# Two-block transformer net on one core: two more granules in the mixer's filler, raw room opened before the up projection, and reciprocal roots taken in twos

## The chip, the cores and the metric

One core of one Trainium2 chip runs the whole program as one kernel. The metric is the device time of one execution in microseconds (us). The engines are TensorE (PE, its weight loads PEld), VectorE (DVE), ScalarE (ACT), GpSimd (POOL) and SyncE (SP), whose queue issues the transfers.

## What is computed

Two blocks on x of 1024 tokens by 1024 columns, in fp32. The change touches the first block, from the mixer's output to the gate behind the MLP:

```
mixed = (gate_attn * y_attn + gate_conv * y_conv) @ w_o
x = x + rms_norm(mixed, g_post_mix)
h = rms_norm(x, g_pre_mlp)
f = square(relu(h @ w_up)) @ w_down          # 1024 -> 4096 -> 1024
x = x + rms_norm(f, g_post_mlp)
x = x + sigmoid(rms_norm(x, g_ple) @ w_ple_gate) * (p @ w_ple_proj)
```

with rms_norm(x, g) = x * rsqrt(mean(x * x) + 1e-6) * g. Before it stand attention, a short convolution and the input projection; behind it a block with memory attention and two mixers. The change leaves their code alone.

## The kernel before

Every fp32 product is three matmuls on rounded halves: an operand is split into hi (ACT, L104 and L112) and lo = x - hi (POOL for weights, L105; DVE for activations, L113), and hi*hi, lo*hi and hi*lo are added in PSUM (L124 to L126). act_hi and act_lo hold the activations of all 1024 tokens. The order of the instructions on each engine isn't written out: a scheduler sets it when the program is built, from the order of the calls, its estimates of durations, and the pools, whose buffers a later tile can have only when the earlier one's readers are done.

**Mixer's way out** (`out_stage`). For each tile of 128 tokens the product with w_o (r_o, L751 to L753), the sum of squares, the reciprocal root, the residual, the next norm, and a transpose on PE (tp, L178) into act_hi and act_lo. A *filler* stands among the last tiles: plain granules of the up projection. A granule is 128 of the 4096 columns; half a granule (j, h) is 24 matmuls on 512 tokens, in ps_f. Half h = 0 needs only tiles 0 to 3, so it can run while tiles 4 to 7 are still normed. Before, the filler is the h = 0 halves of granules 0 and 1.

**Up projection** (`up`). Six more plain halves of granules 0 to 3, then 14 pairs of granules by a scheme of seven products instead of eight (`seven`, in the order 1, 2, 3, 6, 7, 5, 4, each 12 matmuls, in ps_s). Its operands are sums of weight quarters (S, wS_hi, wS_lo, made in `weights`) and of token quarters B: T1, T2, T3 (`token_sums`, DVE operations on 128x2048, made in tiles Tf and split into T_hi and T_lo), and T4 (`last_sum`, made in a tile S and split into B[0, 1]'s own place in act_hi and act_lo). Products 5, 6, 7 and 4 use T1, T2, T3 and T4; products 3 and 7 use the weights' sum S34. ReLU and square give f_out, which goes to DRAM (f_rows_up), one transfer of 128x1024 for each granule.

**Down projection** (`down`). f_raw(j) is loaded from f_rows_up (`load_f`) and split into slot (j + 4) % 8 of act_hi and act_lo, whose token quarters the pairs still read; two granules at a time are multiplied with w_down into ps_d and added to acc. The pool of f_raw, two of 128x1024, is opened with down's other pools, behind those of up.

**Last tiles.** With granules 30 and 31, `after(t)` runs `final(t)`: sum of squares of acc(t) (ACT, L163), reciprocal root q1 (`rstd`, ten DVE operations on 128x1, L143 and L152 to L158), gain (POOL L988, DVE L989), scaling by q1 and adding of x_f (ACT L992, POOL L993, DVE L994); then the sum of squares and the root of the tile t - 1, now with its residual, and its norm xn (L974 to L977), which `turn` transposes for the gate's product (ps_pg).

Of the kernel before, what the change touches and what calls it, by code (L numbers as in the profile page):

```python
# [8 lines left out]
F32 = mybir.dt.float32  # L9
# [3 lines left out]
AF = mybir.ActivationFunctionType  # L13
ALU = mybir.AluOpType
# [14 lines left out]
class Net:  # L29
# [109 lines left out]
    def rstd(self, ss, n):  # L139

        v = self.nc.vector
        x, y, t, u = (self.sm.tile([P, 1], F32, name=f"rstd_{k}") for k in "xytu")
        v.tensor_scalar(out=x, in0=ss, scalar1=1.0 / n, scalar2=EPS, op0=ALU.mult, op1=ALU.add)  # L143
        if self.use_sqrt:
            self.nc.scalar.activation(out=t, in_=ss, func=AF.Sqrt, scale=1.0 / n, bias=self.eps)
            v.reciprocal(out=y, in_=t)
            v.scalar_tensor_tensor(out=t, in0=y, scalar=x, in1=y, op0=ALU.mult, op1=ALU.mult)
            v.tensor_scalar(out=u, in0=t, scalar1=-0.5, scalar2=1.5, op0=ALU.mult, op1=ALU.add)
            v.tensor_tensor(out=y, in0=y, in1=u, op=ALU.mult)
            return y  # L150

        v.tensor_scalar(out=y.bitcast(I32), in0=x.bitcast(I32), scalar1=-0.5, scalar2=float(0x5F3759DF),  # L152
                        op0=ALU.mult, op1=ALU.add)
        for _ in range(2):
            v.scalar_tensor_tensor(out=t, in0=y, scalar=x, in1=y, op0=ALU.mult, op1=ALU.mult)
            v.tensor_scalar(out=u, in0=t, scalar1=0.375, scalar2=-1.25, op0=ALU.mult, op1=ALU.add)
            v.tensor_tensor(out=u, in0=u, in1=t, op=ALU.mult)
            v.scalar_tensor_tensor(out=y, in0=u, scalar=1.875, in1=y, op0=ALU.add, op1=ALU.mult)  # L158
        return y
# [619 lines left out]
    def up(self, st):  # L779


        nc, tc, a = self.nc, self.tc, self.a
        v = nc.vector
        hi, lo = self.act_hi, self.act_lo
        col = lambda k: slice(k * P, (k + 1) * P)
        fp = st.enter_context(tc.tile_pool(name="fo", bufs=1))
        fo = {}

        def leave(j, h):
            if h == 0 or not fo[j][1]:  # L790
                fo[j][1] = True
                return
            nc.sync.dma_start(out=self.fd[j], in_=fo[j][0])

        def out_of(j):
            if j not in fo:
                fo[j] = [fp.tile([P, S], F32, name="f_out", tag=f"f{j % 2}"), False]
            return fo[j][0]

        def plain(j, w, h, psm):  # L800
            ps = psm.tile([P, H], F32, name="ps_f", tag="r")
            self.proj_T(ps, w, col, (hi, lo), 8, h)
            o = out_of(j)[:, h * H:h * H + H]
            nc.scalar.activation(out=o, in_=ps, func=AF.Relu)
            v.tensor_tensor(out=o, in0=o, in1=o, op=ALU.mult)
            leave(j, h)

        def up_w(js):
            return [(j, self.split_w(a["w_up"][j], 1024)) for j in js]

        w01 = []

        def filler(psm):
            w01.extend(up_w([0, 1]))
            for j, w in w01:
                plain(j, w, 0, psm)

        self.out_stage(a["w_o"], a["g_post_mix"], a["g_pre_mlp"], a["x"], self.xd, filler)
# [8 lines left out]
        def rec(out, b):  # L827
            v.tensor_tensor(out=out, in0=b[0].bitcast(F32), in1=b[1].bitcast(F32), op=ALU.add)

        def sub(out, x, y):  # L830
            v.tensor_tensor(out=out, in0=x, in1=y, op=ALU.subtract)

        def token_sums():

            with tc.tile_pool(name="tf", bufs=1) as tf:
                f1, f2, f3 = (tf.tile([P, 4, H], F32, name=f"Tf{n}") for n in (1, 2, 3))
                rec(f1, B[0, 0])
                rec(f3, B[0, 1])
                sub(f1, f3, f1)
                self.split(*T[1], f1)  # L840
                rec(f2, B[1, 1])
                sub(f3, f2, f3)
                sub(f2, f2, f1)
                self.split(*T[2], f2)
                self.split(*T[3], f3)

        def last_sum():

# [28 lines left out]

        def seven(j, ops):

            o11, o12, o21, o22 = (out_of(j + i)[:, h * H:h * H + H] for i in range(2) for h in range(2))  # L880
            k1, u2 = (kp.tile([P, H], F32, name=n) for n in ("k1", "u2"))
            ps = {}

            def add(out, n, more):
                v.tensor_tensor(out=out, in0=ps[n], in1=more, op=ALU.add)

            def done(o, i):
                v.scalar_tensor_tensor(out=o, in0=o, scalar=0.0, in1=o, op0=ALU.max, op1=ALU.mult)
                leave(j + i, 1)

            for n in (1, 2, 3, 6, 7, 5, 4):
                ps[n] = psm.tile([P, H], F32, name=f"ps_s{n}", tag="r")
                (sh, sl), a0, (mh, ml) = ops[n]
                self.mm3(ps[n], [((sh[:, col(a0 + k)], sl[:, col(a0 + k)]), (mh[:, k], ml[:, k])) for k in range(4)])
                if n == 1:
                    nc.scalar.activation(out=k1, in_=ps[n], func=AF.Copy)
                elif n == 2:
                    add(o11, 2, k1)
                    done(o11, 0)
                elif n == 6:  # L900
                    add(u2, 6, k1)
                elif n == 7:
                    add(o21, 7, u2)
                elif n == 5:
                    add(o12, 5, u2)
                    add(o22, 5, o21)
                    add(o12, 3, o12)
                    done(o22, 1)
                    done(o12, 0)
                elif n == 4:  # L910
                    add(o21, 4, o21)
                    done(o21, 1)

        w23 = up_w([2, 3])
        pairs = list(range(4, 32, 2))
        plains = [(j, w, 1) for j, w in w01] + [(j, w, h) for h in range(2) for j, w in w23]
        for n, (j, w, h) in enumerate(plains):
            plain(j, w, h, psm)
            if n == 0:
                token_sums()  # L920
        kp = st.enter_context(tc.tile_pool(name="kept", bufs=2))
        sf = st.enter_context(tc.tile_pool(name="sf", bufs=1))
        wu = st.enter_context(tc.tile_pool(name="wu", bufs=2))
        ahead = weights(4)
# [7 lines left out]
    def mlp(self):  # L932
# [4 lines left out]
        act = (hi, lo)  # L937
        col = lambda k: slice(k * P, (k + 1) * P)
        self.fd = self.dram.tile([32, P, S], F32, name="f_rows_up")
        with ExitStack() as st:  # L940
            self.up(st)
        with ExitStack() as st:
            f2 = st.enter_context(tc.tile_pool(name="f2", bufs=2))
            fp = st.enter_context(tc.tile_pool(name="fp", bufs=2))
            fs = {}
# [678 lines left out]
```

## Time and profile before

| | |
|---|---|
| median of three runs | 2968.9 us (2965.43 to 2971.95) |
| the profiled execution | 2973.59 us |
| its span, first to last instruction | 2971.8 us |
| mean granted TensorE clock | 0.972 of full speed |
| busy: PE, PEld, DVE, ACT, POOL | 93%, 78%, 57%, 41%, 34% |
| moved by DMA | 311.14 MB, 105 GB/s in the mean |

Times within a row of the timeline are counted from the span's start. A matmul is listed with its own length, in which the next one already runs, so the pace is read from start to start. "[2.22 <-DVE act_lo L113]" behind an instruction is the idle time of its engine before it and what ended it. The granted clock of a stretch is 1.00 at 2.4 GHz and 0.50 at 1.2 GHz.

### The profile page before, as it was taken

The page shows a single profiled execution, that of the slowest core. Times are in us where ns is not written, and L with a number is a line of the kernel's source. Part 1 is how long each engine was busy: PE and PEld are TensorE (multiplying, and loading weights), DVE is VectorE, ACT ScalarE, POOL GpSimd, SP SyncE. Part 2 cuts the span into 40 slices and gives each one's busy share as a digit, 9 for nine tenths or more (in the row PEclk, how much of TensorE's full clock was granted, in tenths as well). Part 3 has the DMA queues.
Part 4 walks back from the last instruction along what each step waited for, and adds up shares of the span by engine and source line. Part 5 has one row for each costly group of instructions (what it writes and reads, how often), then busy time and mean ns, then how long its engine had stood idle before and what let it go on. Part 6 is the DMA issues. An engine that isn't in the chain of part 4 may idle for free. (4 is left out here: it accounts for less than half of the span.)

```text
span 2971.8 us, 37779 instructions
## 1 busy us (share of the span) xinstructions
PE 2774.5 (93%) x13490; PEld 2312.0 (78%) x13490; DVE 1692.0 (57%) x3201; ACT 1218.9 (41%) x2368; POOL 995.9 (34%) x823
## 2 busy tenths in 40 slices
PE   7999999998999998999989899689989999999988
PEld 5888778877878887888867689677768978778867
DVE  6320288845387665666587435287872426666643
ACT  5111266642442222121144423377763535555543
POOL 4221111113345442223255212332324344455442
PEclk9999999998999999999989899799999999999999
DMA  5111211127323335323123322632344232222162
GB/s 206 50 44 63 75 56 55 61 70 263 109 77 122 108 106 193 108 90 109 43 82 144 116 87 71 184 116 92 112 142 168 99 112 65 72 72 73 49 234 93
DMA packets 130644, 311.14 MB, mean 105 GB/s; under 512 B 14796, under 2 KB 34892, under 8 KB 130456
## 3 DMA queue, kind: packets, MB, share of 16 engines
q1 hardware_dynamic: 130456, 308.72, 31.0%
q8 instruction: 107, 1.75, 0.2%
q14 instruction: 81, 0.66, 0.1%
HBM read 213.33 MB, written 85.38 MB: 101 GB/s over the span
## 5 line engine op out<-in xcount | busy, mean ns | idle before, releaser
L105 POOL TENSOR_TENSOR w_lo<-w_raw,w_hi 128x1024 fp32r<-128x1024 f32 (+5 forms) x220 | 452.8, 2067 | 1057.8 <-ACT w_hi L104 1055.6
L104 ACT ACTIVATE w_hi<-w_raw 128x1024 fp32r<-128x1024 f32 (+5 forms) x220 | 192.5, 886 | 407.2 <-PE ps L125 90.7
L124 PE MATMUL ps_m<-act_hi,w_hi 128*128 128x512 f32 x716 | 289.8, 405 | 28.6 <-ACT w_hi L104 11.6
L125 PE MATMUL ps_m<-act_lo,w_hi 128*128 128x512 f32 x716 | 283.9, 397 | 0.0
L126 PE MATMUL ps_m<-act_hi,w_lo 128*128 128x512 f32 x716 | 282.4, 396 | 0.0
L113 DVE TENSOR_TENSOR pl<-tp_at,ph 128x512 fp32r<-128x512 f32 (+3 forms) x416 | 222.8, 560 | 85.9 <-ACT ph L112 83.8
L112 ACT ACTIVATE ph<-tp_at 128x512 fp32r<-128x512 f32 (+3 forms) x416 | 196.8, 500 | 106.2 <-PE tp_at L299 95.8
L1017 DVE TENSOR_TENSOR acc<-ps_d,acc 128x512 f32<-128x512 f32 x240 | 161.9, 687 | 109.7 <-PE ps_d L126 109.7
L299 PE MATMUL tp_at<-ident,p 128*128 128x128 f32 x1280 | 204.2, 275 | 16.1 <-DVE pl L113 5.7
L254 ACT ACTIVATE p<-p,mx 128x256 f32<-128x256 f32 (+7 forms) x256 | 180.3, 706 | 81.9 <-DVE mx L243 50.3
L124 PE MATMUL ps_d<-w_hi,act_hi 128*128 128x512 f32 x512 | 202.4, 395 | 7.7 <-ACT act_hi L112 7.7
L125 PE MATMUL ps_d<-w_lo,act_hi 128*128 128x512 f32 x512 | 202.0, 395 | 0.0
L126 PE MATMUL ps_d<-w_hi,act_lo 128*128 128x512 f32 x512 | 199.4, 392 | 0.0
L299 PEld LDWEIGHTS tp_at<-ident,p 128*128 128x128 f32 x1280 | 152.1, 140 | 48.5 <-DVE pl L113 9.1
L124 PEld LDWEIGHTS ps_m<-act_hi,w_hi 128*128 128x128 f32 x716 | 136.8, 191 | 64.8 <-ACT w_hi L104 12.7
L751 PE MATMUL r_o<-w_hi,act_hi 128*128 128x512 f32 x384 | 151.1, 403 | 20.5 <-DVE ga L687 7.9
L126 PEld LDWEIGHTS ps_m<-act_hi,w_lo 128*128 128x128 f32 x716 | 136.0, 190 | 28.6
L125 PEld LDWEIGHTS ps_m<-act_lo,w_hi 128*128 128x128 f32 x716 | 136.9, 191 | 25.9
L291 PE MATMUL o_ps<-ph,v 128*128 128x512 f32 (+3 forms) x400 | 145.5, 364 | 8.5 <-ACT ph L112 4.3
L753 PE MATMUL r_o<-w_hi,act_lo 128*128 128x512 f32 x384 | 151.7, 396 | 0.0
L752 PE MATMUL r_o<-w_lo,act_hi 128*128 128x512 f32 x384 | 151.3, 396 | 0.0
L292 PE MATMUL o_ps<-pl,v 128*128 128x512 f32 (+3 forms) x400 | 146.7, 374 | 0.4 <-DVE pl L113 0.2
(389 smaller groups left out, 6938.1 us busy)
## 6 DMA issues: line engine op xcount, KB each, us to landing
w_raw<-in_w_in SPq DMA_DIRECT2D x40, 512.0 KB, 3.4
w_raw<-in_w_up SPq DMA_DIRECT2D x32, 512.0 KB, 3.9
f_rows_up<-f_out SPq DMA_DIRECT2D x32, 512.0 KB, 5.4
w_raw<-in_w_down SPq DMA_DIRECT2D x32, 512.0 KB, 4.4
f_raw<-f_rows_up SPq DMA_DIRECT2D x32, 512.0 KB, 3.8
xd<-x_o SPq DMA_DIRECT2D x16, 512.0 KB, 2.7
w_raw<-in_w_out SPq DMA_DIRECT2D x16, 512.0 KB, 8.6
x_o<-xd SPq DMA_DIRECT2D x16, 512.0 KB, 4.8
```

Source lines behind the costliest of these rows:

```text
L104: nc.scalar.activation(out=hi[:, sl], in_=raw, func=AF.Copy)
L105: nc.gpsimd.tensor_tensor(out=lo[:, sl], in0=raw, in1=hi[:, sl].bitcast(F32), op=ALU.subtract)
L112: nc.scalar.activation(out=hi, in_=src, func=AF.Copy)
L113: nc.vector.tensor_tensor(out=lo, in0=src, in1=hi.bitcast(F32), op=ALU.subtract)
L124: nc.tensor.matmul(out, lhsT=sh, rhs=mh, start=(i == 0), stop=False)
L125: nc.tensor.matmul(out, lhsT=sh, rhs=ml, start=False, stop=False)
L126: nc.tensor.matmul(out, lhsT=sl, rhs=mh, start=False, stop=(i == n - 1))
L254: nc.scalar.activation(out=p[:, :nk], in_=p[:, :nk], func=AF.Exp, scale=-1.0, bias=mx[:, 0:1], accum_out=it["sum"][:, j:j + 1])
L299: nc.tensor.transpose(tp[:, j * P:(j + 1) * P], it["p"][j][:, k * P:(k + 1) * P], self.ident)
L752: nc.tensor.matmul(r, lhsT=a, rhs=wl, start=False, stop=False)
L753: nc.tensor.matmul(r, lhsT=b, rhs=wh, start=False, stop=(k == 7))
L1017: nc.vector.tensor_tensor(out=acc[:, t, sl], in0=ps, in1=acc[:, t, sl], op=ALU.add)
```

## The change

1. The filler takes the h = 0 halves of granules 0 to 3 (96 matmuls, before 48); behind the mixer's way out stand the four h = 1 halves. The call of `token_sums` stands ahead of them, not behind the first. It does with two tiles Tf instead of three, in seven sums and differences of 128x2048 besides the splits, before six. f_out is a tile of 128x512, four of them, and each half goes to DRAM by itself (64 transfers of 256 KB for 32 of 512 KB). k1 and u2 have one buffer each, before two.
2. The pool of f_raw is opened ahead of `up`.
3. `final(t)` for t from 1 to 7 takes the sums of squares of acc(t) and acc(t - 1) into the two columns of one tile and one root of both: twelve operations on 128x2, before two chains of ten on 128x1.

```diff
@@ rstd
-        x, y, t, u = (self.sm.tile([P, 1], F32, name=f"rstd_{k}") for k in "xytu")
+        w = ss.shape[-1]
+        x, y, t, u = (self.sm.tile([P, w], F32, name=f"rstd{'' if w == 1 else w}_{k}", bufs=6 if w == 1 else 2) for k in "xytu")
...
-            v.scalar_tensor_tensor(out=t, in0=y, scalar=x, in1=y, op0=ALU.mult, op1=ALU.mult)
+            if ss.shape[-1] == 1:
+                v.scalar_tensor_tensor(out=t, in0=y, scalar=x, in1=y, op0=ALU.mult, op1=ALU.mult)
+            else:
+                v.tensor_tensor(out=t, in0=y, in1=y, op=ALU.mult)
+                v.tensor_tensor(out=t, in0=t, in1=x, op=ALU.mult)
@@ up
-        fp = st.enter_context(tc.tile_pool(name="fo", bufs=1))
+        fp = st.enter_context(tc.tile_pool(name="fo", bufs=4))
...
+            nc.sync.dma_start(out=self.fd[j, :, h * H:h * H + H], in_=fo.pop((j, h)))
...
-            w01.extend(up_w([0, 1]))
-            for j, w in w01:
+            first.extend(up_w(range(4)))
+            for j, w in first:
                 plain(j, w, 0, psm)
...
-                f1, f2, f3 = (tf.tile([P, 4, H], F32, name=f"Tf{n}") for n in (1, 2, 3))
+                f1, f2 = (tf.tile([P, 4, H], F32, name=f"Tf{n}") for n in (1, 2))
                 rec(f1, B[0, 0])
-                rec(f3, B[0, 1])
-                sub(f1, f3, f1)
+                rec(f2, B[0, 1])
+                sub(f1, f2, f1)
                 self.split(*T[1], f1)
-                rec(f2, B[1, 1])
-                sub(f3, f2, f3)
-                sub(f2, f2, f1)
-                self.split(*T[2], f2)
-                self.split(*T[3], f3)
+                for n, f in ((3, f2), (2, f1)):
+                    sub(f, B[1, 1][0].bitcast(F32), f)
+                    v.tensor_tensor(out=f, in0=f, in1=B[1, 1][1].bitcast(F32), op=ALU.add)
+                    self.split(*T[n], f)
...
-        plains = [(j, w, 1) for j, w in w01] + [(j, w, h) for h in range(2) for j, w in w23]
-        for n, (j, w, h) in enumerate(plains):
-            plain(j, w, h, psm)
-            if n == 0:
-                token_sums()
-        kp = st.enter_context(tc.tile_pool(name="kept", bufs=2))
+        token_sums()
+        for j, w in first:
+            plain(j, w, 1, psm)
+        kp = st.enter_context(tc.tile_pool(name="kept", bufs=1))
@@ mlp
-        with ExitStack() as st:
-            self.up(st)
-        with ExitStack() as st:
+        with tc.tile_pool(name="fr", bufs=2) as fr, ExitStack() as st:
+            with ExitStack() as s2:
+                self.up(s2)
...
-                raw = f3.tile([P, S], F32, name="f_raw")
+                raw = fr.tile([P, S], F32, name="f_raw")
...
-                    q1 = self.rstd(self.sumsq(acc[:, t, :], junk()), D)
+                    ss = self.sm.tile([P, 2 if t else 1], F32, name="ss2" if t else "ss", bufs=2 if t else None)
+                    for i in range(2 if t else 1):
+                        nc.scalar.activation(out=junk(), in_=acc[:, t - i, :], func=AF.Square, accum_out=ss[:, i:i + 1])
+                    qs = self.rstd(ss, D)
+                    q1, q = qs[:, 0:1], qs[:, 1:2] if t else None
...
-                q = self.rstd(self.sumsq(acc[:, t - 1, :], junk()), D) if t else None
+                else:
+                    q = self.rstd(self.sumsq(acc[:, t - 1, :], junk()), D)
```

How the built order moves, at the places that matter below.

The vector engine's queue around the last act_lo of the mixer's way out (act_lo<-tp), before. Tf are the token sums' tiles, T_lo their splits, f_out<-f_out the squares of plain halves, S the weights' sums of the first pair.

```order
544 L828 TENSOR_TENSOR Tf_6891<-act_hi,act_lo 128x2048
545 L113 TENSOR_TENSOR act_lo<-tp,act_hi 128x4x128 x2
546 L828 TENSOR_TENSOR Tf_6893<-act_hi,act_lo 128x2048
547 L828 TENSOR_TENSOR Tf_6892<-act_hi,act_lo 128x2048
548 L831 TENSOR_TENSOR Tf_6891<-Tf_6893,Tf_6891 128x2048
549 L831 TENSOR_TENSOR Tf_6893<-Tf_6892,Tf_6893 128x2048
550 L113 TENSOR_TENSOR T_lo<-Tf_6891,T_hi 128x2048
551 L831 TENSOR_TENSOR Tf_6892<-Tf_6892,Tf_6891 128x2048
552 L805 TENSOR_TENSOR f_out<-f_out 128x512
553 L113 TENSOR_TENSOR T_lo<-Tf_6893,T_hi 128x2048
554 L805 TENSOR_TENSOR f_out<-f_out 128x512
555 L113 TENSOR_TENSOR T_lo<-Tf_6892,T_hi 128x2048
```

The same place now, from the last act_lo to the last T_lo:

```order
547 L113 TENSOR_TENSOR act_lo<-tp,act_hi 128x4x128 x2
548 L829 TENSOR_TENSOR Tf_6927<-act_hi,act_lo 128x2048
549 L832 TENSOR_TENSOR Tf_6926<-Tf_6927,Tf_6926 128x2048
550 L832 TENSOR_TENSOR Tf_6927<-act_hi,Tf_6927 128x2048
551 L113 TENSOR_TENSOR T_lo<-Tf_6926,T_hi 128x2048
552 L844 TENSOR_TENSOR Tf_6927<-Tf_6927,act_lo 128x2048
553 L832 TENSOR_TENSOR Tf_6926<-act_hi,Tf_6926 128x2048
554 L806 TENSOR_TENSOR f_out<-f_out 128x512
555 L113 TENSOR_TENSOR T_lo<-Tf_6927,T_hi 128x2048
556 L844 TENSOR_TENSOR Tf_6926<-Tf_6926,act_lo 128x2048
557 L806 TENSOR_TENSOR f_out<-f_out 128x512
558 L113 TENSOR_TENSOR T_lo<-Tf_6926,T_hi 128x2048
```

Behind the last act_lo stand nine operations of 128x2048 where eight stood, and the last T_lo's Tf is finished one operation before it. One Tf stands ahead of that act_lo, as before.

The vector engine's queue where up ends, before. ps_s with u and f_out are the adds of products 7, 5 and 3; the last add of a pair, of product 4, is o21.

```order
756 L885 TENSOR_TENSOR f_out<-ps_s_8862,f_out 128x512
757 L888 SCALAR_TENSOR_TENSOR f_out<-f_out 128x512 x2
758 L885 TENSOR_TENSOR f_out<-ps_s_8922,f_out 128x512
759 L888 SCALAR_TENSOR_TENSOR f_out<-f_out 128x512
760 L113 TENSOR_TENSOR act_lo<-f_raw,act_hi 128x1024 x2
```

And now:

```order
754 L113 TENSOR_TENSOR act_lo<-f_raw,act_hi 128x1024 x2
755 L885 TENSOR_TENSOR u_8897<-ps_s_8941,k_8896 128x512
756 L113 TENSOR_TENSOR act_lo<-f_raw,act_hi 128x1024
757 L885 TENSOR_TENSOR f_out<-ps_s_8955,u_8897 128x512
758 L113 TENSOR_TENSOR act_lo<-f_raw,act_hi 128x1024
759 L885 TENSOR_TENSOR f_out<-ps_s_8969,u_8897 128x512
760 L885 TENSOR_TENSOR f_out<-ps_s_8969,f_out 128x512
761 L885 TENSOR_TENSOR f_out<-ps_s_8928,f_out 128x512
762 L888 SCALAR_TENSOR_TENSOR f_out<-f_out 128x512
763 L113 TENSOR_TENSOR act_lo<-f_raw,act_hi 128x1024
764 L888 SCALAR_TENSOR_TENSOR f_out<-f_out 128x512
765 L885 TENSOR_TENSOR f_out<-ps_s_8989,f_out 128x512
```

The splits of f_raw(0) and (1), and those of (2), (3) and (4), which load into the same two tiles, stand among the last pair's adds, ahead of the one of product 4 (row 765).

The vector engine's queue in the last tiles now, one whole chain between two tiles:

```order
856 L159 TENSOR_TENSOR rstd_t<-rstd_y 128x2
857 L113 TENSOR_TENSOR act_lo<-tp,act_hi 128x4x128
858 L160 TENSOR_TENSOR rstd_t<-rstd_t,rstd_x 128x2
859 L161 TENSOR_SCALAR rstd_u<-rstd_t 128x2
860 L990 TENSOR_TENSOR acc<-acc,gain 128x512
861 L162 TENSOR_TENSOR rstd_u<-rstd_u,rstd_t 128x2
862 L113 TENSOR_TENSOR act_lo<-tp,act_hi 128x4x128
863 L163 SCALAR_TENSOR_TENSOR rstd_y<-rstd_u,rstd_y 128x2
```

and at about the same place before:

```order
866 L156 TENSOR_SCALAR rstd_u<-rstd_t 128x1
867 L974 SCALAR_TENSOR_TENSOR xn<-acc,rstd_y,gain 128x512
868 L157 TENSOR_TENSOR rstd_u<-rstd_u,rstd_t 128x1
869 L143 TENSOR_SCALAR rstd_x<-ss 128x1
870 L158 SCALAR_TENSOR_TENSOR rstd_y<-rstd_u,rstd_y 128x1
871 L152 TENSOR_SCALAR rstd_y<-rstd_x 128x1
872 L155 SCALAR_TENSOR_TENSOR rstd_t<-rstd_y,rstd_x 128x1 x2
873 L156 TENSOR_SCALAR rstd_u<-rstd_t 128x1 x2
```

Two chains ran interleaved; now one runs by itself, with larger operations in between.

## Rows read from the trace of the kernel before

**Rows 1.** The page's busy shares (us busy, share of the span, instructions) and its DMA issues (KB each, median us from issue to landing).

```profile
PE 2774.5 (93%) x13490; PEld 2312.0 (78%) x13490; DVE 1692.0 (57%) x3201; ACT 1218.9 (41%) x2368; POOL 995.9 (34%) x823
...
f_raw<-f_rows_up SPq DMA_DIRECT2D x32, 512.0 KB, 3.8
```

**Rows 2.** PE's waits between 820 and 1600 us: line and tile that waited, what it waited for, us in total, times, longest.

```profile
PE tp L178 <- DVE xn L974: 11.1, 2, 10.8
PE ps_pg L124 <- ACT act_hi L112: 7.8, 3, 3.8
PE ps_d L124 <- ACT act_hi L112: 7.7, 1, 7.7
PE tp L178 <- DVE act_lo L113: 2.3, 2, 1.5
PE ps_f L124 <- DVE act_lo L113: 2.2, 1, 2.2
...
PE tp L178 <- DVE rstd_u L148: 0.9, 1, 0.9
```

**Rows 3.** A table of stretches: us from and to, length, busy us and instructions of PE, PE's weight loads, vector, scalar and Pool engine, granted TensorE clock, DMA share, GB/s.

```profile
827.00:853.00 26.00, 20.58 (x91) 16.15 (x90) 24.26 (x41) 11.90 (x24) 8.86 (x6) 0.87 0.22 82
853.00:882.00 29.00, 29.00 (x129) 24.01 (x129) 24.77 (x15) 12.53 (x13) 11.96 (x5) 1.00 0.21 73
...
1148.60:1160.00 11.40, 3.69 (x9) 2.81 (x9) 5.62 (x6) 3.17 (x3) 3.51 (x2) 0.63 0.97 370
1500.00:1520.00 20.00, 12.53 (x51) 10.13 (x52) 18.55 (x58) 11.19 (x20) 11.05 (x8) 0.67 0.24 80
...
1507.30:1587.10 79.80, 69.96 (x299) 55.92 (x299) 68.33 (x174) 37.79 (x62) 44.37 (x30) 0.88 0.25 86
```

**Rows 4.** PE's timeline on the mixer's way out and through the plain granules: start us, us, engine, line, operation. ps_f are plain granules, the first ps_s is the first pair.

```profile
827.38 0.40 PE L124 MATMUL ps_f<-act_hi,w_hi 128*128 128x512 f32 x1
...
848.24 0.63 PE L125 MATMUL ps_f<-act_lo,w_hi 128*128 128x512 f32 x1
848.66 0.63 PE L126 MATMUL ps_f<-act_hi,w_lo 128*128 128x512 f32 x1
...
851.20 0.40 PE L126 MATMUL ps_f<-act_hi,w_lo 128*128 128x512 f32 x1
...
882.06 0.39 PE L124 MATMUL ps_s<-act_hi,w_hi 128*128 128x512 f32 x1
```

**Rows 5.** PE's timeline in the MLP's last tiles: the last ps_d before the first transposes, the first transposes, the last group of transposes and the matmul behind it.

```profile
1496.13 0.39 PE L126 MATMUL ps_d<-w_hi,act_lo 128*128 128x512 f32 x1
1507.32 1.11 PE L178 MATMUL tp<-ident,xn 128*128 128x128 f32 x4 [10.80 <-DVE xn L974]
...
1586.71 0.60 PE L178 MATMUL tp<-ident,xn 128*128 128x128 f32 x4
1587.07 0.48 PE L124 MATMUL ps_pg<-w_hi,act_hi 128*128 128x512 f32 x1
```

**Rows 6.** All engines and SyncE's queue where up ends and down begins.

```profile
1148.39 0.39 PE L126 MATMUL ps_s<-act_hi,wE_lo 128*128 128x512 f32 x1
1148.81 0.82 SPq L961 DMA_DIRECT2D f_raw<-f_rows_up  x2
...
1150.47 0.68 DVE L885 TENSOR_TENSOR f_out<-ps_s,f_out 128x512 f32<-128x512 f32 x1
...
1155.38 2.21 ACT L112 ACTIVATE act_hi<-f_raw 128x1024 fp32r<-128x1024 f32 x2 [4.11 <-DMA f_raw<-f_rows_up]
...
1156.49 0.79 PE L124 MATMUL ps_d<-w_hi,act_hi 128*128 128x512 f32 x1 [7.71 <-ACT act_hi L112]
```

**Rows 7.** The vector engine's timeline on the mixer's way out and through the plain granules. Tf and T_lo belong to the token sums, S<-w_raw to the weights' sums of the first pair.

```profile
844.12 2.27 DVE L828 TENSOR_TENSOR Tf<-act_hi,act_lo 128x2048 f32<-128x2048 f32 x1
...
847.52 4.47 DVE L828 TENSOR_TENSOR Tf<-act_hi,act_lo 128x2048 f32<-128x2048 f32 x2
...
858.64 4.49 DVE L831 TENSOR_TENSOR Tf<-Tf,Tf 128x2048 f32<-128x2048 f32 x1
...
868.78 0.69 DVE L868 TENSOR_TENSOR S<-w_raw 128x512 f32<-128x512 f32 x1
...
872.40 0.69 DVE L831 TENSOR_TENSOR S<-w_raw,S 128x512 f32<-128x512 f32 x1
```

**Rows 8.** The Pool and the scalar engine on the same stretch: w_lo of granules 2 and 3, w_lo of the first pair, wS_hi, and T4's act_hi.

```profile
824.20 4.75 POOL L105 TENSOR_TENSOR w_lo<-w_raw,w_hi 128x1024 fp32r<-128x1024 f32 x2 [2.42 <-ACT w_hi L104]
...
857.22 3.77 POOL L874 TENSOR_TENSOR w_lo<-w_raw,w_hi 128x1024 fp32r<-128x1024 f32 x1 [14.17 <-ACT w_hi L873]
...
872.40 2.01 ACT L873 ACTIVATE wS_hi<-S 128x1024 fp32r<-128x1024 f32 x2 [2.99 <-DVE S L831]
...
889.38 1.92 ACT L112 ACTIVATE act_hi<-S 128x2048 fp32r<-128x2048 f32 x1 [5.81 <-DVE S L831]
```

**Rows 9.** The vector engine in the last tiles: two small operations of a chain behind one another (timeline), the group of one such operation with two inputs (busy us, mean ns | idle before), and the second half of the scaled tiles (first and last start).

```profile
1501.48 0.16 DVE L157 TENSOR_TENSOR rstd_u<-rstd_u,rstd_t 128x1 f32<-128x1 f32 x1
1501.67 0.16 DVE L158 SCALAR_TENSOR_TENSOR rstd_y<-rstd_u,rstd_y 128x1 f32<-128x1 f32 x1
...
L157 DVE TENSOR_TENSOR rstd_u<-rstd_u,rstd_t 128x1 f32<-128x1 f32 x30 | 11.5, 385 | 0.1
...
L994 DVE SCALAR_TENSOR_TENSOR acc<-acc,rstd_y,x_f x8: 737/750/752, 1497.3 to 1568.0; 128x512 f32<-128x512 f32 x8
```

More of the change, by code (lines that the diff above doesn't have):

```diff
@@ L785, in up, with out_of @@
         col = lambda k: slice(k * P, (k + 1) * P)
-        fp = st.enter_context(tc.tile_pool(name="fo", bufs=1))
+        fp = st.enter_context(tc.tile_pool(name="fo", bufs=4))
         fo = {}
         def leave(j, h):
[L790 to L798, printed above, removed]
+            nc.sync.dma_start(out=self.fd[j, :, h * H:h * H + H], in_=fo.pop((j, h)))
+        def out_of(j, h):
+            fo[j, h] = fp.tile([P, H], F32, name="f_out")
+            return fo[j, h]
         def plain(j, w, h, psm):
@@ L802, in plain @@
             self.proj_T(ps, w, col, (hi, lo), 8, h)
-            o = out_of(j)[:, h * H:h * H + H]
+            o = out_of(j, h)
             nc.scalar.activation(out=o, in_=ps, func=AF.Relu)
@@ L809, in up_w @@
             return [(j, self.split_w(a["w_up"][j], 1024)) for j in js]
-        w01 = []
+        first = []
         def filler(psm):
-            w01.extend(up_w([0, 1]))
-            for j, w in w01:
+            first.extend(up_w(range(4)))
+            for j, w in first:
                 plain(j, w, 0, psm)
@@ L878, in seven @@
         def seven(j, ops):
-            o11, o12, o21, o22 = (out_of(j + i)[:, h * H:h * H + H] for i in range(2) for h in range(2))
+            o11, o12, o21, o22 = (out_of(j + i, h) for i in range(2) for h in range(2))
             k1, u2 = (kp.tile([P, H], F32, name=n) for n in ("k1", "u2"))
@@ L885, in add, with done @@
                 v.tensor_tensor(out=out, in0=ps[n], in1=more, op=ALU.add)
-            def done(o, i):
+            def done(o, i, h):
                 v.scalar_tensor_tensor(out=o, in0=o, scalar=0.0, in1=o, op0=ALU.max, op1=ALU.mult)
-                leave(j + i, 1)
+                leave(j + i, h)
             for n in (1, 2, 3, 6, 7, 5, 4):
@@ L898, in seven @@
                     add(o11, 2, k1)
-                    done(o11, 0)
+                    done(o11, 0, 0)
                 elif n == 6:
@@ L907, in seven @@
                     add(o12, 3, o12)
-                    done(o22, 1)
-                    done(o12, 0)
+                    done(o22, 1, 1)
+                    done(o12, 0, 1)
                 elif n == 4:
                     add(o21, 4, o21)
-                    done(o21, 1)
-        w23 = up_w([2, 3])
+                    done(o21, 1, 0)
         pairs = list(range(4, 32, 2))
-        plains = [(j, w, 1) for j, w in w01] + [(j, w, h) for h in range(2) for j, w in w23]
-        for n, (j, w, h) in enumerate(plains):
-            plain(j, w, h, psm)
-            if n == 0:
-                token_sums()
-        kp = st.enter_context(tc.tile_pool(name="kept", bufs=2))
+        token_sums()
+        for j, w in first:
+            plain(j, w, 1, psm)
+        kp = st.enter_context(tc.tile_pool(name="kept", bufs=1))
         sf = st.enter_context(tc.tile_pool(name="sf", bufs=1))
```

## The prediction

> **What bounds the kernel now.** I read the page's busy shares first: PE works 93% of the span, the vector engine, next behind it, 57% [rows 1]. So time can only come out of PE's own stops and of the half clock behind them. PE's waits between 820 and 1600 us give the three places that the change touches: the mixer's way out (2.2 us on act_lo before the first plain granule, 3.2 before transposes), the step from up to down (7.7 us on act_hi of f_raw), and the MLP's last tiles (11.1 us on xn, 7.8 on act_hi) [rows 2]. The table of stretches shows that a stop is dearer than its wait: the granted clock is 0.87, 0.63 and 0.88 there, and 1.00 where PE runs through [rows 3].
>
> I price each place as elapsed time less work. At full clock a matmul takes 0.227 us: 136 of them from 851.20 to 882.06; at the half clock, 1.2 of 2.4 GHz, 0.42 (848.24 to 848.66) [rows 4]. A group of four transposes takes 0.36 (1586.71 to 1587.07) [rows 5].
>
> - **Mixer's way out.** From the filler's first matmul, 827.38, to the pairs' first, 882.06, are 54.7 us [rows 4]. The work is 192 x 0.227 + 6 x 0.36 = 45.7. **Lost: 9.0.**
> - **Up to down.** The last pair ends at about 1148.6; PE starts again at 1156.49 [rows 6], and its first 12 matmuls run at half clock (12 x 0.2 = 2.5). **Lost: 10.4.**
> - **Last tiles.** PE stops at 1496.5 and starts at 1507.32. From there to 1587.07 it issues 237 matmuls and 16 groups of transposes, 59.5 us of work in 79.8 [rows 5]. **Lost: 10.8 + 20.3 = 31.**
>
> **The change, part by part.** PE's matmuls are as many as before, so nothing but these losses can move.
>
> *Four granules as filler.* Before, the filler's 48 matmuls run out with four groups of transposes still to come; PE stops before three of them and then 2.2 us for the last act_lo [rows 2]. With 96 spread among them the filler reaches 827.38 + 96 x 0.227 + 6 x 0.36 = 851.3, and the three small stops go. The last stop stays: a Tf sum of 2.27 us stands ahead of the last act_lo in the vector queue [rows 7] and still does, now with f_out squares beside it. Taking 2.2 us again, and 8 matmuls at half clock (1.6), the 96 that are left end at 851.3 + 2.2 + 1.6 + 21.8 = 876.9, 5.2 earlier than 882.06.
>
> That makes the token sums late. Products 6, 7 and 5 of the first pair use T2, T3 and T1, product 4 uses T4, which is made from T2, and the weights' sums for product 3 stand behind them all in the vector queue. Behind the last act_lo nine operations of 128x2048 stand where eight stood. Nine at 2.2 (two took 4.47) are 19.8; two f_out squares 1.2; the last split waits 1.9 for its T_hi, whose Tf is now finished last; and a vector operation with two SBUF inputs stretches beside the Pool's (one sub took 4.49 beside w_lo's 3.77) [rows 7, 8]: one such hold, 2.2. Sum 25.1, so the last T_lo ends at 853.5 + 25.1 = 878.6, against 868.8. The S sums of the weights follow in the same queue (868.78 to 873.1, 4.3 us [rows 7]), then two wS_hi (2.0 [rows 8]): wS_hi for product 3 is there at 884.9. PE wants it at 876.9 + 24 x 0.227 = 882.4: **a new stop of 2.5 us**. T4_hi, the scalar engine's split, ended at 891.3 [rows 8], 18.2 behind the S sums; the same chain gives 901 now, less up to 3 since fewer f_out squares stand between. PE comes to product 4 after 72 matmuls, at 884.9 + 10.9 = 895.8. I take T4 at 899.5, and 1.7 for half clock behind that stop. The ideal for that point is 873.1 + 16.3 = 889.4, so 11.8 are lost where 9.0 were: **+3**. Bounds: only the stop at act_lo is left, 3.8 lost, -5; one more hold of the Pool's length in each chain, +7.
>
> The Trainium skill ("SBUF — State Buffer", Who interferes with whom) says that a vector instruction with two SBUF inputs and a GpSimd instruction that reads SBUF exclude each other, each for the other's whole length, whichever starts first. The 4.49 beside 3.77 agrees. By that rule any of the nine sums could be held, and the term would be nearer its upper bound; the row has one such meeting in 21 us, and I keep +3.
>
> f_out in halves doubles the writes, 32 to 64 of half the size. The DMA share in the plain granules is 0.21 [rows 3] and nothing on PE waits for them: nothing. One k1 and one u2 instead of two are read before the next pair writes them: nothing.
>
> *Raw room opened ahead.* f_raw(0) and f_raw(1) land during up, so the scalar engine's 4.11 us of waiting for them go [rows 6]. But the first ps_d needs a PSUM bank that the pairs leave: that of the last product 4, freed by its o21 add. That add stood right behind PE (1150.47). Now act_lo of f_raw(2), (3) and (4) stand ahead of it in the vector queue, and f_raw(4) may load only when act_lo(2) has freed its room. Counted from the last pair's start: product 3 frees act_hi's slot at 8.2; act_lo(0) ends at 10.6, act_lo(1) at 11.8; f_raw(2), landing 3.8 behind its issue [rows 1], is there at 14.5; act_lo(2) ends at 16.8; f_raw(4) lands at 20.7; act_hi(4) 21.8; act_lo(4), beside the Pool's w_lo, 24; the o21 add 24.9. The pair itself ends at 19.05. So PE starts 5.9 behind it, not 7.9, with the same half clock: **-2**. Bounds: everything on time, -8; both rounds of f_raw landing in 6.6, as the first did (1148.81 to 1155.38 [rows 6]), 5.6 later, +4.
>
> *Two roots per chain.* Seven chains of twelve small operations stand for fourteen of ten: 56 fewer on the vector engine, at 0.19 from start to start [rows 9] 10.6 us. In this stretch it is busy 68.3 of 79.8 us, in its first quarter 18.55 of 20 [rows 3], and a small operation with two inputs takes 0.385 in the mean where 0.16 is its own time [rows 9]. This is the one place where the vector engine sets PE's stops. The first xn comes about when it did. Behind it PE has more other work between the turns; from the places of transposes and xn in the queues I count stops of 0.7, 0.4, 0.9, 2.2 and 1.1 = 5.3, and 30 matmuls at half clock, 6.0: 59.5 + 11.3 = 70.8 where it was 79.8, -9. The pairs of turns behind it wait in part for the same queues and may give 1 us back: **-8**. Bounds: -20, only the first stop left; +6, the ring told of below.
>
> **Sum:** +3 - 2 - 8 = -7. On the profiled execution, 2973.6 us, that is 2966.6; this execution lies 4.7 above the median of the three runs, 2968.9, so in runs **2962**. About 0.2%, 6 us, is what a measurement of this kernel can tell from no change; the forecast lies just past it.
>
> **Rivals.**
> 1. *All three stops close.* -5, -8 and -12: 2944. For it: each edit aims at the longest wait of its place. Against: the vector queue, in which the sums stand one behind another. 0.12.
> 2. *Stops only move.* +3 and -2 as above, and the last tiles no faster, since the Pool's part of each turn (44.4 of 79.8 us [rows 3]) and x_f in one buffer stay in the path: 2970. 0.26.
> 3. *Slower by a ring in the last tiles.* The new root of tile t needs the sum of squares of tile t-1 after its scaling and adding. So chain, scale, Pool add, square and chain again form a ring: 12 x 0.19 for the chain and some 5 for the rest, 7.4 us a turn with the queues free. The eight scaled tiles came 1497.3 to 1568.0 [rows 9], 10.1 a turn, without that ring. If the queues bring it past 11, seven turns end 6 us later than before: +3 - 2 + 6 = +7, 2976. It decides from there on. 0.14. The Trainium skill ("VectorE: DVE Perf Modes", The TRN2 errata) speaks for this rival: a vector operation pays a fixed cost whatever its width, so twelve narrow ones are slower than ten for the tile that waits, by 0.4 us a turn at this row's spacing. No row here has two columns.
> 4. *The change doesn't do what it says:* granules 2 and 3 aren't split in time, and the filler stands. Their w_lo ran from 824.20 to 828.95 before [rows 8], well ahead; 2969. 0.03.
>
> The forecast has 0.45, its own range 2956 to 2967. The range over the cases is 2947 to 2975. Faster by over 0.2%: rival 1 and most of the 0.45, 0.49. Slower by over 0.2%: rival 3 and a little of the others, 0.16. The rest, 0.35, is within.
>
> **What would show it.** No wait of PE among the filler's transposes, but one of about 2 us on the last act_lo; new stops at the first pair's products 3 and 4, on wS_hi and on T4's act_hi; PE's first ps_d released by the o21 add 5 to 7 us behind the last pair; the last tiles 8 to 10 us shorter, with less half clock. I am wrong in a term if PE runs into the first pairs without a stop, if ps_d starts under 3 us behind the pairs, or if the scaled tiles come further apart than 10.1 us.

## The result and the profile after

Slower: 2993.7 us median of four runs (2992.25 to 2996.91) against 2967.16 of before, ratio 1.0098 (95% interval 1.0082 to 1.0114): 26.5 us between the medians, some 29 by the ratio. The forecast was 2962, the range ended at 2975. The profiled execution took 2992.25 us, its span is 2990.5.

The waits that were foretold are there. PE's waits from 830 to 1650 us (line and tile that waited, what it waited for, us in total, times, longest), the answer to [rows 2]:

```profile
PE tp L183 <- DVE xn L971: 9.3, 1, 9.3
PE ps_d L124 <- DVE f_out L885: 5.3, 1, 5.3
PE ps_s L124 <- ACT act_hi L112: 4.6, 1, 4.6
PE ps_pg L126 <- DVE act_lo L113: 4.3, 1, 4.3
PE ps_f L124 <- DVE act_lo L113: 3.8, 1, 3.8
...
PE ps_s L124 <- ACT wS_hi L873: 2.3, 2, 1.4
```

The ps_d wait fell from 7.7 to 5.3 and is now released by the o21 add; ps_s waits on wS_hi and on T4's act_hi, which it did not before. In all the waits up to the last tiles are much what they were: 40.6 us before (815 to 1650 us), 42.6 now (830 to 1672). But PE's busy time rose from 2774.5 to 2802.2 us with the same 13490 matmuls: the time isn't in the waits. A table of one stretch shows it best, 100 to 300 us, the input projection, code that no line of the change touches (us from and to, length, busy us and instructions of PE, PEld, DVE, ACT, POOL, granted clock, DMA share, GB/s). Before:

```profile
100.00:300.00 200.00, 200.00 (x879) 164.59 (x878) 42.09 (x49) 32.67 (x45) 37.09 (x20) 1.00 0.15 50
```

After:

```profile
100.00:300.00 200.00, 200.00 (x862) 161.70 (x861) 41.39 (x48) 32.42 (x44) 37.16 (x20) 1.00 0.15 50
```

PE is busy all the time at a granted clock of 1.00 in both, and issues 862 matmuls where it issued 879. **Each matmul takes 0.232 us instead of 0.2275, with no wait and no half clock.** The *pace* is the time from start to start of neighbouring rows of PE's timeline, with waits and half clock left out. By stage, in the mean:

| pace, us | before | after |
|---|---|---|
| ps (input projection) | 0.2280 | 0.2325 |
| ps_m (second block) | 0.2291 | 0.2335 |
| r_o (both ways out) | 0.2269 | 0.2312 |
| ps_f (plain granules) | 0.2274 | 0.2334 |
| ps_s (pairs) | 0.2267 | 0.2308 |
| ps_d (down) | 0.2267 | 0.2289 |
| ps_pg (gate) | 0.2281 | 0.2294 |
| ps_ad (second block) | 0.2269 | 0.2333 |

Multiplied by the matmuls of these stages (1152, 2148, 1152, 192, 1176, 1536, 384, 480) the differences make 33 us, somewhat more than the 27.7 by which PE's busy time rose. Where the rest is saved was not traced.

What had changed for the matmuls is where their operands lie. In the built program each small tile takes 32 B a partition in SBUF. The change adds ten (rstd2_x, _y, _t, _u and ss2, two buffers each): 320 B. act_hi and act_lo lie ahead of them and stay, all weights lie behind them and move. Before, act_hi, act_lo and nearly all weights lay at the same place modulo 256 B (their address divided by 256 leaves 160); after, the weights are at 224. These are addresses in the built program; the trace doesn't list them.

### The profile page after: what moved, and what is told of

It reads as the page before. It is cut to its first block, busy times and chain, and to the rows that moved or that the text cites. A ratio compares the mean times of both kernels' runs of the same rounds, so it can differ in the third digit from the quotient of the medians.

```text
span 2990.5 us, 37804 instructions
## 1 busy us (share of the span) xinstructions
PE 2802.2 (94%) x13490; PEld 2309.4 (77%) x13490; DVE 1690.9 (57%) x3146; ACT 1217.3 (41%) x2368; POOL 1000.8 (33%) x823
```

## The experiments

Three theories for the loss: A, the place of the tiles sets the pace; B, the edits and their order cost it; C, it is the chip or the day. For the edits themselves the terms of the prediction stand to be tried. Each time is given against runs of before that were taken with it. A *pad* is a wider constant tile ahead of everything that moves; it adds no instruction, and the order of every engine is the same with it.

**e1: the kernel before, tiles moved by 320 B.**

```diff
-        bg = self.bg = self.const.tile([P, 16], F32, name="bg")
+        bg = self.bg = self.const.tile([P, 96], F32, name="bg")[:, :16]
```

> The kernel before, with one constant tile widened by 320 B a partition and nothing else: every instruction in the same order, only the places of the SBUF tiles behind that tile move by 320 B, as in the changed kernel; act_hi and act_lo stay. Theory A (places): the matmuls' pace hangs on where weights lie against the activations, so the paces of the changed kernel come back (0.2325 in the input projection ps, 0.231 in r_o and ps_s, where before has 0.227 to 0.228), about 27 us in all: 2994, ratio 1.009. Theory B (edits): the loss comes from the edits' own waits and another order; then this is 2967, ratio 1.000, pace 0.227 everywhere. Theory C (a chip or a day): ratio anywhere, with pace changing in both kernels.

2991.35 us against 2963.29, ratio 1.0103 (1.0082 to 1.0123): as slow as the whole change, by 320 unused bytes. The paces are those of after (ps 0.2326, ps_s 0.2307, ps_d 0.2289, ps_ad 0.2334). The stretch from 100 to 300 us:

```profile
100.00:300.00 200.00, 200.00 (x862) 161.29 (x861) 41.33 (x48) 32.63 (x44) 37.03 (x20) 1.00 0.15 50
```

862 again. B and C fall.

**e2: the change, tiles moved on by 192 B** (512 in all), by a bg of [P, 64].

> The changed kernel, with the same constant tile widened by 192 B, so that its small new tiles and the pad make 512 B and every weight tile lies as before modulo 256. Theory A: pace back to 0.227 in all stages, some 27 us less than the changed kernel: 2967, ratio to before 0.998 to 1.001, what is left being the edits: about +6 at the mixer's way out and the first pairs, -2.4 at up to down, -4 in the last tiles. Theory B: no change against the changed kernel, ratio 1.010.

2962.9 against 2963.29, ratio 1.0003 (0.9993 to 1.0014). All paces of before are back:

```profile
100.00:300.00 200.00, 200.00 (x879) 164.59 (x878) 42.09 (x49) 32.66 (x45) 37.08 (x20) 1.00 0.15 50
```

So the three edits together are worth nothing that can be measured, and the places cost all that was lost. What the edits do shows here undisturbed; PE's waits from 815 to 1200 us:

```profile
PE ps_d L124 <- DVE f_out L885: 5.7, 1, 5.7
PE ps_s L124 <- ACT act_hi L112: 4.7, 1, 4.7
PE ps_f L124 <- DVE act_lo L113: 3.8, 1, 3.8
PE ps_s L124 <- ACT wS_hi L873: 2.2, 2, 1.3
```

**e9, e10, e8, e11: the kernel before, tiles moved by 256, 64, 128 and 32 B** (bg of [P, 80], [P, 32], [P, 48], [P, 24]).

> The kernel before, tiles behind one constant moved by 256 B, nothing else: the control of the three moves. If the distance between weights and activations counts modulo 256 B: every pace as before (0.227), ratio 1.000. If any move of the tiles costs: 0.232, ratio 1.01.

Ratio 1.0005 (0.999 to 1.002), all paces as before; 100 to 300 us:

```profile
100.00:300.00 200.00, 200.00 (x879) 164.61 (x878) 42.09 (x49) 32.67 (x44) 37.08 (x20) 1.00 0.16 50
```

> The kernel before, tiles moved by 64 B. Theory of the distance modulo 256: the same paces as with 320 B, stage by stage: ps 0.2325, ps_f 0.2335, ps_d 0.229, ps_ad 0.2333, about 2991. If only the absolute size of the move matters, less than with 320.

One run, 2996.85. The paces are those of 320 B: ps 0.2325, ps_f 0.2333, ps_d 0.2289, ps_ad 0.2333:

```profile
100.00:300.00 200.00, 200.00 (x862) 161.74 (x861) 41.82 (x49) 32.64 (x44) 37.14 (x20) 1.00 0.15 50
```

> The kernel before, weights moved by 128 B against act_hi and act_lo, nothing else. Read for the pace in stages where the moving operand is an activation and the stationary one a weight (ps, ps_ad), and the reverse (ps_d, r_o). If only being apart matters: 0.2325 as with 320 B. If it goes by the distance modulo 256, 128 is a distance of its own, the same in both directions: one pace for ps and ps_d. If the distance modulo 128 counts: 0.2267, as before.

One run, 3005.08. One pace in both directions: ps 0.2323, ps_d 0.2324, r_o 0.2324:

```profile
100.00:300.00 200.00, 200.00 (x863) 161.81 (x862) 42.12 (x49) 32.53 (x44) 37.15 (x20) 1.00 0.15 50
```

> The kernel before, tiles moved by 32 B. The theory has no value for this distance yet; between 0.2267 and 0.2335 if the loss grows with the distance, 0.232 at once if any distance that isn't a multiple of 256 costs alike.

One run, 3005.23. ps 0.2327, ps_d 0.2333, r_o 0.2334: at once the whole loss.

Two of the means above, those of ps and ps_s, are mixed. In ps a sixth of the matmuls, and in ps_s the products with T1, T2 and T3, three of seven, have a moving operand that isn't in act_hi or act_lo but lies behind the pad too, so that both operands move alike. This separates the distance of the two operands from the place of one alone. In e1 twelve matmuls that stream T_hi and T_lo and twelve that stream act_hi and act_lo, each time from the first to the one behind the twelfth (the moving operand is named first):

```profile
1006.78 0.39 PE L124 MATMUL ps_s<-T_hi,wS_hi 128*128 128x512 f32 x1
...
1009.50 0.39 PE L124 MATMUL ps_s<-T_hi,wS_hi 128*128 128x512 f32 x1
...
1010.86 0.39 PE L124 MATMUL ps_s<-act_hi,wE_hi 128*128 128x512 f32 x1
...
1013.66 0.39 PE L124 MATMUL ps_s<-act_hi,w_hi 128*128 128x512 f32 x1
```

and the twelve with act_hi before:

```profile
993.58 0.39 PE L124 MATMUL ps_s<-act_hi,wE_hi 128*128 128x512 f32 x1
...
996.30 0.39 PE L124 MATMUL ps_s<-act_hi,w_hi 128*128 128x512 f32 x1
```

The twelve with T take 2.72 us, as they did before; those with act_hi take 2.80 where they took 2.72. Over all pairs the pace with T is 0.2267 before and 0.2272 in e1, with act_hi and act_lo 0.2267 and 0.2333. So the weights' new place costs next to nothing where the other operand moved with them: what counts is the distance of the two.

Together, by the distance of the stationary operand from the moving one, modulo 256 B, for the matmuls that have act_hi or act_lo as one operand. In ps, ps_m, ps_f, ps_ad and these products of ps_s the weights stand still in the array and move by the pad; in ps_d, ps_pg and r_o they stream, so a pad of 64 is a distance of 192.

| distance, B | 0 | 32 | 64 | 128 | 192 | 224 |
|---|---|---|---|---|---|---|
| pace, us | 0.2267 to 0.2286 | 0.2331 to 0.2334 | 0.2331 to 0.2333 | 0.2323 to 0.2333 | 0.2289 to 0.2316 | 0.2332 to 0.2334 |
| stages, run | all, before | weights still, e11 | weights still, e1 and e10 | all, e8 | weights stream, e1 and e10 | weights stream, e11 |

**e3: the filler's part alone** (as in the diff of `up`; no new small tiles, so no pad).

> The kernel before with the first part alone: four granules as filler, token sums in two tiles, f_out in halves; tiles lie as before modulo 256. My own term: the two new stops at the first pair's products 3 and 4 cost more than the filler saves; in the changed kernel they were 2.3 and 4.6 us with half clock behind them: +4 to +6, ratio 1.0015 to 1.002. Rival: this part carries most of the 27 us lost, ratio 1.007 or more. Second rival: the filler's gain holds and the stops are small, -3 to -5, ratio 0.999.

2974.49, ratio 1.0035 (1.0021 to 1.0048), slower by 10 us: more than my term, less than the first rival. The same two stops as in e2 (4.7 on act_hi, 1.0 on wS_hi). The wait before down is longer too, 9.1 us where before has 7.7: f_raw's first load is issued 2.0 us behind the last pair's last matmul, before 0.4. I had put f_out in halves at nothing; whether it is the cause was not tried alone.

**e4: two roots alone, pad of 192 B** (as in the diff of `rstd` and `final`).

> The kernel before with the third part alone (two roots per chain), and a pad of 192 B so that tiles lie as before modulo 256. My term: -4 to -8 in the last tiles, ratio 0.9975 to 0.9987. Rival (ring): the new root of one tile waits for the one before it, +6, ratio 1.002. Second rival: no change, the vector engine isn't what holds the tiles.

2965.03, ratio 1.0006 (0.9997 to 1.0015): nothing, though the vector engine has 56 operations less. The eight scaled tiles (first and last start):

```profile
L1004 DVE SCALAR_TENSOR_TENSOR acc<-acc,rstd_y,x_f x8: 742/752/752, 1498.8 to 1569.1; 128x512 f32<-128x512 f32 x8
```

10.0 us a turn where [rows 9] has 10.1. Two later stops of PE:

```profile
1566.83 0.80 PE L126 MATMUL ps_pg<-w_hi,act_lo 128*128 128x512 f32 x1 [4.92 <-DVE act_lo L113]
...
1645.10 0.69 PE L183 MATMUL tp<-ident,xn 128*128 128x128 f32 x2 [9.66 <-DVE act_lo L113]
```

The gate's first turns end sooner (first ps_pg to last ps_d 39.9 us, before 45.0), and in this execution what they gain is given back in these two stops (4.9 us; 9.7 where before had 6.05).

**e5: raw room alone.** The pool is opened ahead of `up`; for its room the token sums use two tiles and k1, u2 one buffer.

```diff
+        with tc.tile_pool(name="fr", bufs=2) as fr, ExitStack() as st:
+            with ExitStack() as s2:
+                self.up(s2)
...
+                raw = fr.tile([P, S], F32, name="f_raw")
```

> The kernel before with the raw room opened ahead of up; to make room for it the token sums use two tiles and k1, u2 one buffer, as in the changed kernel, but the filler, the plain granules and f_out stay. My term: PE's idle time between up and down falls from 7.7 to about 5.7 us, released by the o21 add, ratio 0.999 to 0.9995. Rival (by the difference of the runs so far, whole change less its two other parts): -8 to -11, ratio 0.9965. Second rival: the one more token sum brings stops into the first pairs, ratio 1.001 or more.

2967.12 against 2971.03, ratio 0.9991 (0.9976 to 1.0007). PE's wait between up and down is 5.1 us, on the o21 add; last ps_s to first ps_d 5.5 us, before 8.1. My term; the one more token sum brings no stop into the pairs while the old filler stands.

**e6: the change with pad, granules 4 and 5 plain too.**

```diff
-        pairs = list(range(4, 32, 2))
+        more = up_w([4, 5])
+        pairs = list(range(6, 32, 2))
...
+        for j, w in more:
+            for h in range(2):
+                plain(j, w, h, psm)
...
-        ahead = weights(4)
+        ahead = weights(6)
```

> The changed kernel with the pad of 192 B and granules 4 and 5 done plain too, between the token sums and the pairs (13 pairs instead of 14): 96 matmuls for the 84 of a pair, 2.7 us more work. If the two new stops at products 3 and 4 are lateness of the vector engine's sums, the 21.8 us of cover take both away with their half clock: 9.3 less and 2.7 more, about 2957, ratio to before 0.998. Rival: the sums are held by something that also moves with the granules (f_out squares, the Pool), the stops stay, ratio 1.001.

2959.58 against 2971.03, ratio 0.9966 (0.9952 to 0.9979), faster than both kernels. PE's waits from 815 to 920 us:

```profile
PE ps_f L124 <- DVE act_lo L113: 3.8, 1, 3.8
PE tp L183 <- DVE act_lo L113: 3.0, 1, 3.0
```

Both stops at the pairs are gone: they were lateness of the sums, which 21.8 us of cover take away, and not something that moves along with the granules. The wait before the first h = 1 half stays, and one of 3.0 at a transpose stands where e2 had none.

**e7: raw room and two roots, old filler, pad.**

> Second and third part together without the filler's (raw room ahead, two roots per chain, pad of 192 B). If the parts add up: raw room -2, roots +1, ratio 0.9995. If the raw room is worth more in company, 0.997.

2972.75 against 2971.03, ratio 1.0002 (0.999 to 1.0015). No more than the parts.

**e12: filler, raw room and six plain granules, single roots, no pad.**

> Filler and raw room with two more plain granules (13 pairs), without the two roots per chain, so that no pad is needed. If the roots give nothing: as with them, ratio 0.996 to 0.9975. If the roots were worth 3 to 4 us in company of the others: 0.998. If they cost: 0.995.

2960.09 against 2969.26, ratio 0.9967 (0.9955 to 0.998): the roots give nothing here either.

By stage, from the first starts in PE's timeline of each profiled execution (us; the 94 to 96 from the first r_o to the first ps_f are left out):

| | before | change | e2 | e3 | e4 | e5 | e6 | e12 |
|---|---|---|---|---|---|---|---|---|
| start to r_o | 733.3 | 744.3 | 733.3 | 737.2 | 735.5 | 735.6 | 735.2 | 733.1 |
| first ps_f to first ps_s | 54.7 | 52.8 | 53.0 | 52.9 | 54.5 | 54.7 | 78.0 | 78.0 |
| pairs | 266.3 | 280.4 | 275.6 | 276.2 | 266.3 | 266.3 | 247.3 | 247.3 |
| last ps_s to first ps_d | 8.1 | 5.7 | 6.1 | 9.5 | 7.9 | 5.5 | 6.2 | 6.2 |
| first ps_d to first ps_g | 487.2 | 487.0 | 483.3 | 488.0 | 488.7 | 487.1 | 486.3 | 485.1 |
| from there to the end | 1328.1 | 1324.3 | 1313.9 | 1322.2 | 1320.6 | 1328.6 | 1310.2 | 1306.9 |

In the last row all run nearly the same order, and still single executions differ: e9, the very order of before at the same places modulo 256, took 1320.0 there against 1328.1, with a mean granted clock of 0.974 over its span against 0.972. So parts are compared by stage and whole kernels by their ratios. The two don't quite agree for e6 and e12: by stage the filler and the pairs take 4.3 us more than before (2.7 of it work), the step to down 1.9 less, the rest up to ps_g 0.9 to 2.1 less, so that they should run level; the ratios say 10 us less. The last row can't place that gain, since e2, whose ratio is 1.0003, is as short there within 3.7 us of e6. What the runs do show is the clock. In the mean over its runs the granted clock is 0.9756 in e6 and 0.9752 in e12, and 0.9723 and 0.9722 in the runs of before beside them; 0.003 of 2960 us is some 9 us, an estimate that takes lost clock for lost time. A part of it is the half clock behind the two stops that are gone. Where the rest comes from is open.

## Why the prediction was wrong

**The step that failed** is the first of "The change part by part": "PE's matmuls are as many as before, so nothing but these losses can move." As many they are, but most of them take up to 2.9% longer (0.2333 us for 0.2267), over the whole program. e1 and e2 show the cause from both sides: 320 unused bytes make before as slow as the change, 192 more bring the change back level. I read the small tiles of `rstd` as two columns for one and didn't ask what lies behind them. Neither side of the range allowed for a pace of its own.

The Trainium skill ("SBUF — State Buffer", Who interferes with whom) says that PE never waits on anyone, its moving operand and its weight load having ports of their own. The measurement differs: 0.2267 against 0.2333 us a matmul with nothing but the distance of these two operands changed. Why the distance modulo 256 B matters, these runs don't show.

Of the terms, with the places made equal (e2, and the part alone):

- *Filler: foretold +3 (-5 to +7), measured +7.6 by stage in e2, +8.1 and a ratio of +10 us in e3.* The mechanism was right, its size wrong. PE's timeline of the change, first filler matmul, first h = 1 half, first pair, its products 3 and 4:

```profile
840.28 0.39 PE L124 MATMUL ps_f<-act_hi,w_hi 128*128 128x512 f32 x1
...
869.28 0.79 PE L124 MATMUL ps_f<-act_hi,w_hi 128*128 128x512 f32 x1 [3.80 <-DVE act_lo L113]
...
893.12 0.39 PE L124 MATMUL ps_s<-act_hi,w_hi 128*128 128x512 f32 x1
...
900.25 0.50 PE L124 MATMUL ps_s<-act_hi,wS_hi 128*128 128x512 f32 x1 [1.36 <-ACT wS_hi L873]
...
916.16 0.50 PE L124 MATMUL ps_s<-act_hi,wE_hi 128*128 128x512 f32 x1 [4.63 <-ACT act_hi L112]
```

The vector engine's from the last act_lo on, and the scalar engine's T_hi, wS_hi and T4's act_hi:

```profile
867.94 1.28 DVE L113 TENSOR_TENSOR act_lo<-tp,act_hi 128x512 fp32r<-128x512 f32 x2
...
878.19 4.49 DVE L844 TENSOR_TENSOR Tf<-Tf,act_lo 128x2048 f32<-128x2048 f32 x1
...
891.88 2.29 DVE L113 TENSOR_TENSOR T_lo<-Tf,T_hi 128x2048 fp32r<-128x2048 f32 x1 [1.38 <-ACT T_hi L112]
...
894.69 0.68 DVE L868 TENSOR_TENSOR S<-w_raw 128x512 f32<-128x512 f32 x1
```

```profile
889.93 1.92 ACT L112 ACTIVATE T_hi<-Tf 128x2048 fp32r<-128x2048 f32 x1 [4.81 <-DVE Tf L844]
...
897.70 1.06 ACT L873 ACTIVATE wS_hi<-S 128x1024 fp32r<-128x1024 f32 x1 [2.38 <-DVE S L832]
...
899.14 1.05 ACT L873 ACTIVATE wS_hi<-S 128x1024 fp32r<-128x1024 f32 x1
...
914.20 1.91 ACT L112 ACTIVATE act_hi<-S 128x2048 fp32r<-128x2048 f32 x1 [9.96 <-DVE S L832]
```

From the last act_lo's end, 869.2, to the last T_lo's end, 894.2, are 25.0 us; foretold 25.1, with one hold by the Pool (4.49). The stop at product 3 was foretold as 2.5; it is 1.4, and 0.9 in the second pair (0.9 and 1.3 in e2). But the wait before the h = 1 half is 3.8, not 2.2, since a Tf (2.29) and an f_out square stand before the last act_lo, and 13 matmuls run at half clock behind it in e2, not 8. T4's act_hi ends 75.8 us behind the filler's start, not 72.1, and costs 4.6 instead of 3.7.
- *Raw room: foretold -2, measured -2.0 in e2 and -2.6 in e5.* PE starts 5.5 us behind the last pair, foretold 5.9, and the rows are those of the step:

```profile
1173.36 1.06 ACT L112 ACTIVATE act_hi<-f_raw 128x1024 fp32r<-128x1024 f32 x1 [1.34 <-DMA f_raw<-f_rows_up]
1173.55 0.40 PE L126 MATMUL ps_s<-act_hi,wE_lo 128*128 128x512 f32 x1
...
1174.58 3.37 DVE L113 TENSOR_TENSOR act_lo<-f_raw,act_hi 128x1024 fp32r<-128x1024 f32 x1
...
1175.87 1.06 ACT L112 ACTIVATE act_hi<-f_raw 128x1024 fp32r<-128x1024 f32 x1 [1.45 <-DMA f_raw<-f_rows_up]
...
1178.47 0.68 DVE L885 TENSOR_TENSOR f_out<-ps_s,f_out 128x512 f32<-128x512 f32 x1
...
1179.07 1.21 DVE L113 TENSOR_TENSOR act_lo<-f_raw,act_hi 128x1024 fp32r<-128x1024 f32 x1
...
1179.29 0.76 PE L124 MATMUL ps_d<-w_hi,act_hi 128*128 128x512 f32 x1 [5.35 <-DVE f_out L885]
```

The pair's last matmul is issued at 1173.55. act_lo of f_raw(3) takes 3.37 beside the Pool's splits, the o21 add follows only at 1178.47, and PE starts at once. Of the 7.7 us of waiting 5.3 remain, on another releaser.
- *Two roots: foretold -8, measured nothing* (e4 1.0006; -4 by stage in e2, +1.5 in e4). PE's first turns in e4 end sooner, but the scaled tiles are still 10.0 us apart (10.2 in the change), and the later turns give it back. So 56 operations less in the vector engine's queue don't move the end: that is the time of rival 2 for this part, while its reason, the Pool's part of each turn and x_f's one buffer, was not tried. The ring of rival 3 did not reach its point, 11 us a turn. The small operations are hardly dearer for the second column: 0.20 from start to start, 0.16 each, in e4:

```profile
1502.08 0.17 DVE L153 TENSOR_SCALAR rstd_y<-rstd_x 128x2 int32<-128x2 int32 x1
1502.28 0.16 DVE L159 TENSOR_TENSOR rstd_t<-rstd_y 128x2 f32<-128x2 f32 x1
1502.48 0.16 DVE L160 TENSOR_TENSOR rstd_t<-rstd_t,rstd_x 128x2 f32<-128x2 f32 x1
1502.68 0.17 DVE L161 TENSOR_SCALAR rstd_u<-rstd_t 128x2 f32<-128x2 f32 x1
...
1503.67 1.22 DVE L162 TENSOR_TENSOR rstd_u<-rstd_u,rstd_t 128x2 f32<-128x2 f32 x1
```

and the one with two inputs lasts as long as the Pool's operation beside it (1503.10 to 1504.87), 1.22 us here and 0.47 in the mean, before 0.385.

By stage, with +7.6, -2.0 and -4.0, the edits come to +1.7 us; measured +0.9 (e2). That is closer than it deserves: the -4.0 is one execution, in a stage where e9 with the order of before was 2.3 shorter too. By the ratios of the parts alone the sum is +10.4 - 2.7 + 1.8 = +9.5, and why the three together cost 8.6 less than that stays open. The sum of the forecast, -7, was 8 us too good against e2, and the pace, not foreseen at all, added 28.

## What to carry to other kernels

Ask of a change what it does to the place of everything behind it, even if it adds but some bytes; compare the addresses of the moving and the stationary operands before and after, modulo 256 B, and give a change that adds small tiles a pad of its own before it is judged. If PE's busy time rises with as many matmuls, a full clock and no waits, look there first: count matmuls in a stretch that the change doesn't touch. And a filler closes one wait but makes what it delays late: the work that feeds the next stage must have cover of its own, as e6's two granules gave.

## What the runs showed of the hardware that was not expected

- A matmul of 512 columns, at a granted clock of 1.00 and with a weight load for each, takes 0.2267 us (ps_s and ps_d before) if its stationary and moving operand lie at the same place modulo 256 B in SBUF, and 0.229 to 0.2333 if they do not; 32 B are enough for the whole loss (e11), 256 B cost nothing (e9).
- A tensor_scalar on one column wasn't held by the Pool in the last tiles, on two columns it was. Before (busy us, mean ns | idle before), and e4:

```profile
L143 DVE TENSOR_SCALAR rstd_x<-ss 128x1 f32<-128x1 f32 x14 | 2.0, 146 | 2.2 <-ACT junk_f L163 2.2
L152 DVE TENSOR_SCALAR rstd_y<-rstd_x 128x1 int32<-128x1 int32 x14 | 2.0, 145 | 0.1
```

```profile
L162 DVE TENSOR_TENSOR rstd_u<-rstd_u,rstd_t 128x2 f32<-128x2 f32 x14 | 6.5, 468 | 0.3
...
L153 DVE TENSOR_SCALAR rstd_y<-rstd_x 128x2 int32<-128x2 int32 x7 | 5.5, 785 | 0.2
...
L144 DVE TENSOR_SCALAR rstd_x<-ss 128x2 f32<-128x2 f32 x7 | 3.0, 433 | 4.7 <-ACT junk_f L994 4.6
```

0.146 and 0.145 us on one column, 0.433 and 0.785 in the mean on two, 0.17 where alone. It isn't that the narrow ones met no Pool: in before, 15 tensor_scalar on one column started while a Pool operation ran, and none took over 0.154 us; in e4 eight on two columns did, and six of them took 0.5 to 2.3. The Trainium skill ("SBUF — State Buffer", Who interferes with whom) says that tensor_scalar in a two-port mode contends with GpSimd and outside it doesn't, which would fit; that the width is what switches the mode was not tried by itself.
